# Four ordinary chunks in every Strassen block, and low-weight products behind high-weight ones

## The chip, the cores and the metric

The kernel runs on one core of a Trainium2 chip. The metric is the device time of one execution in microseconds. In the profile PE is TensorE (matmuls), PEld its weight loads, DVE is VectorE, ACT is ScalarE, and SP is the engine whose queue issues the DMAs.

## The reference

A two-layer encoder trunk on 256 tokens of width 2048, all in float32. Each layer has a token mixer (dilated and grouped-query attention in layer 0, latent attention in layer 1) and a channel mixer. Each sub-layer is added to x after a second norm. What matters here is the channel mixer, whose last product is the down projection, 256 x 5632 by 5632 x 2048:

```python
D_MODEL = 2048
SEQ = 256
D_FF = 5632
...
def conv_glu(h, w_up, conv_w, conv_b, w_down):
    u = h @ w_up
    gate, val = u[..., :D_FF], u[..., D_FF:]
    gate = depthwise_conv3(gate, conv_w, conv_b)
    return (jax.nn.gelu(gate, approximate=False) * val) @ w_down
...
    for i in range(DEPTH):
        p = layers[i]
        h = rms_norm(x, p['mix_pre'])
        if i % 2 == 0:
            m = mixer_dilated_gqa(h, *p['mixer'], pos, row, col)
        else:
            m = mixer_mla(h, *p['mixer'], pos)
        x = x + rms_norm(m, p['mix_post'])
        h = rms_norm(x, p['ffn_pre'])
        x = x + rms_norm(conv_glu(h, *p['ffn']), p['ffn_post'])
    return x
```

## The kernel before

**Numbers in two parts.** TensorE multiplies a rounded format, so each float32 operand is held as a high part (its rounding) and a low part (the rest). A product of two such operands is three matmuls into one PSUM bank: high by high, high by low, low by high. `mm3` (lines 227 to 232) issues them: line 230 multiplies the activation's high part by the weight's high part, line 231 the activation's high part by the weight's low part, line 232 the activation's low part by the weight's high part. In the down projection the activations are the stationary operand (128 x 128) and the weights the moving one (512 columns).

**The stream of weights.** All weights of the program form one list of chunks of 128 x 1024 (512 KB), in the order in which they are used. `weights` (line 187) hands out the next chunk, splits up to two chunks further (`_split`, line 159) and loads up to five ahead (`_load`, line 148). A split is a cast on ACT (line 173, `whi`) and, after it, a subtraction on DVE (line 174, `wlo`). There are four buffers for the loaded chunk (`raw`) and three each for `whi` and `wlo`. All loads are issued from SP's queue.

**The down projection** (`down`, lines 1002 to 1129) makes the 2048 output columns in two halves `h`, and each half as two column blocks `o` of 512 by two token halves `t` of 128: four banks of accumulation (`acc`). Along the 5632 rows there are 22 pairs of 256 rows. The pairs from 6 on are done in the ordinary way: one chunk for each pair and `o`, with two row blocks and two token halves, so four products, 12 matmuls. The first six pairs (`PAIRS`) are done by a Strassen scheme: for one pair the 2 x 2 blocks of tokens, rows and columns take seven products instead of eight. Its weights come as two chunks (`seven_a`, `seven_b`, one buffer each), and are used in four steps j = 0 to 3 with 2, 2, 2 and 1 products (6, 6, 6 and 3 matmuls). Step 0 splits `seven_a` as it came. Behind it four subtractions on DVE (`Seven.sums`, line 68, with line 76) turn `seven_a` and `seven_b` in place into differences and fill `seven_t`; step 1 splits the new `seven_a`, step 2 the new `seven_b`, step 3 `seven_t`. The next pair's `seven_a` can be loaded once step 1 has been split, its `seven_b` once step 2 has. The seven sums go to the four ordinary banks and to four more (`at`); at the end of the six pairs `added` and `done` bring them together on ACT and DVE. The sums of tokens that the scheme needs are made on DVE by `sums` (line 1010) while the first chunks run.

**The order.** `down_order(h)` writes it out: `LEAD[h]` ordinary chunks first (6 in the first half, 1 in the second), then for each of the six pairs a block with the four steps and some ordinary chunks among them, then the ordinary chunks left over. For pairs 0 to 3 a block is step 0, two ordinary chunks, step 1, an ordinary chunk, steps 2 and 3, an ordinary chunk. For pairs 4 and 5 it is step 0, two ordinary chunks, steps 1 and 2, an ordinary chunk, step 3. The same list orders the loads (`all_chunks`, line 1152). In the second half the last three ordinary chunks (`HOLD`) are held and run first for t = 0 and then for t = 1, so that the norm can begin.

**Who sets the engines' order.** The framework sorts the instructions of each engine when the program is built: it follows the written order, and puts an instruction that it takes for ready ahead of one that it takes for waiting. Products into one bank keep their order. The order on an engine is fixed when the kernel runs.

`products` (line 1095) issues one step's or chunk's products for one token half; for a Strassen step all are issued in the first call.

Of the kernel before, what the change touches and what calls it, by code (L numbers as in the profile page):

```python
# [31 lines left out]


PAIRS = 6
LEAD = 6, 1


def down_order(h):

    plain = [("plain", p, o) for o in range(2) for p in range(PAIRS, KF // 2)]  # L40
    out, plain = plain[:LEAD[h]], deque(plain[LEAD[h]:])
    for p in range(PAIRS):
        for j in (0, None, None, 1, None, 2, 3, None) if p < 4 else (0, None, None, 1, 2, None, 3):
            out.append(plain.popleft() if j is None else ("seven", p, j))
    return out + list(plain)

# [40 lines left out]
class Model:  # L87
# [914 lines left out]
    def down(self, gh, gl, post, pre):  # L1002

        nc = self.nc
        add = lambda out, a, b, op=ALU.add: nc.vector.tensor_tensor(out=out, in0=a, in1=b, op=op)  # L1005
        mm = self.mm3
        ss = self.small.tile([P, 2, 4], F32, tag="ss", name="ss", bufs=2)
        seven, m, gains = [], [], []

        def sums():  # L1010

            for i in range(PAIRS // 2):
                tmp = self.act.tile([P, 2, 1024], F32, tag="xm3", name="sums")
                add(tmp[:, 0], gh[i].rearrange("p k t -> p (k t)").bitcast(F32),
                    gl[i].rearrange("p k t -> p (k t)").bitcast(F32))
                a = tmp[:, 0].rearrange("p (q k t f) -> p q k t f", q=2, k=2, t=2)
                s = tmp[:, 1].rearrange("p (q n f) -> p q n f", q=2, n=4)
                a11, a12, a21, a22 = (a[:, :, k, t] for t in range(2) for k in range(2))
                add(s[:, :, 0], a21, a22)
                add(s[:, :, 1], s[:, :, 0], a11, ALU.subtract)  # L1020
                add(s[:, :, 2], a11, a21, ALU.subtract)
                add(s[:, :, 3], a12, s[:, :, 1], ALU.subtract)
                yield
                seven.append(self.act.tile([P, 2, 4, 2, P], F32R, tag=f"xm{i}", name=f"seven{i}"))
                self.parted(seven[i][:, :, :, 0, :], seven[i][:, :, :, 1, :], s)
                yield

        def tokens(k, t):
            return tuple(g[k // 4][:, k % 4, t * P:(t + 1) * P] for g in (gh, gl))

        def summed(p, n):
            return tuple(seven[p // 2][:, p % 2, n, i, :] for i in range(2))

        def operands(kind, p, j, t):

            if kind == "plain":
                return [(2 * j + t, lambda k=2 * p + i: tokens(k, t), i) for i in range(2)]
            if t:
                return []
            return [[(4, lambda: tokens(2 * p, 0), 0), (0, lambda: tokens(2 * p + 1, 0), 1)],  # L1040
                    [(5, lambda: summed(p, 0), 0), (1, lambda: tokens(2 * p + 1, 1), 1)],
                    [(7, lambda: summed(p, 2), 0), (2, lambda: summed(p, 3), 1)],
                    [(6, lambda: summed(p, 1), 0)]][j]

        def added(h, at):

            p1, p5, p6, p7 = at
            x = m[h]
            nc.scalar.copy(x[:, 0, 0], p1)
            add(x[:, 1, 0], p6, x[:, 0, 0])  # L1050
            yield
            add(x[:, 0, 1], p7, x[:, 1, 0])
            add(x[:, 1, 0], p5, x[:, 1, 0])
            yield
            add(x[:, 1, 1], p5, x[:, 0, 1])
            yield

        def total(h, o, t):
            x = m[h][:, o, t]
            add(x, banks[2 * o + t], x)  # L1060
            return x

        def scaled(h, o, t):
            x = m[h][:, o, t]
            add(x, x, gains[2 * h + o], ALU.mult)

        def done(h, o, first=None):
            if first:
                yield from first
            for t in range(2):  # L1070
                self.square_sums(ss[:, t, 2 * h + o:2 * h + o + 1], total(h, o, t))
                yield
                scaled(h, o, t)
                yield

        gains.append(self.gain_row(post, 0))
        self.now(sums())
        ended = None
        for h in range(2):
            items = down_order(h)  # L1080
            units = [n for n, item in enumerate(items) if item[0] == "seven"]
            if h == 0:
                gains.append(self.gain_row(post, 1))
            n = len(items) - (HOLD if h else 0)
            todo = [(i, t) for i in range(n) for t in range(2)] + \
                [(i, t) for t in range(2) for i in range(n, len(items))]
            used = [(i, t, *op) for i, t in todo for op in operands(*items[i], t)]
            first, last = {}, {}
            for q, u in enumerate(used):
                first.setdefault(u[2], q)  # L1090
                last[u[2]] = q
            used = deque(enumerate(used))
            banks = self.acc(4)

            def products(i, t, w):
                while used and used[0][1][:2] == (i, t):
                    q, (_, _, b, x, blk) = used.popleft()
                    c = slice(512 * blk, 512 * blk + 512)
                    xh, xl = x()
                    mm(banks[b], xh, xl, w[0][:, c], w[1][:, c], q == first[b], q == last[b])  # L1100

            for i in range(n):
                if i == units[0]:
                    banks += [self.psum("at") for _ in range(4)]
                w = self.weights()
                while items[i][0] == "seven" and len(seven) <= items[i][1] // 2:
                    self.tick()
                for t in range(2):
                    products(i, t, w)
                self.tick()  # L1110
                if i == units[-1]:
                    m.append(self.act.tile([P, 2, 2, 512], F32, tag="xm2" if h else "xm3", name=f"m{h}"))
                    if h:
                        gains.append(self.gain_row(post, 3))
                    ended = self.now(done(h, 0, added(h, banks[4:])))
            if h == 0:
                self.finish(ended)
                gains.append(self.gain_row(post, 2))
                ended = self.now(done(0, 1))
                self.finish(ended)  # L1120
                self.table(AF.Sqrt, ss[:, 0, 1:2])
        self.finish(ended)
        part = self.three(ss)
        ws = [self.weights(self.at + HOLD - j) for j in range(HOLD)]
        for t in range(2):
            for j in range(HOLD):
                products(n + j, t, ws[j])
        self.passage([x[:, o] for x in m for o in range(2)], part, lambda t: total(1, 1, t),
                     lambda t: scaled(1, 1, t), pre)
# [22 lines left out]
    def all_chunks(self):  # L1152
        a = self.a
        groups = lambda w, gs: [w[g, c] for g in gs for c in range(w.shape[1])]
        out = groups(a["w_in0"], [8, 6, 7, 0, 2, 4, 1, 3, 5])
        out += [a["w_out0"][g, c] for g in range(4) for c in (4, 5, 6, 7, 0, 1, 2, 3)]

        def down(w):
            items = []
            for h in range(2):  # L1160
                pairs = [Seven(w[2 * h, p], w[2 * h + 1, p]) for p in range(PAIRS)]
                items += [w[2 * h + j, p] if kind == "plain" else (pairs[p], j) for kind, p, j in down_order(h)]
            return items

        ffn = lambda l: groups(a[f"w_up{l}"], [g for j in range(NFG) for g in (j, NFG + j)]) + \
            down(a[f"w_down{l}"])
        out += ffn(0)
        out += groups(a["w_in1"], [0, 1]) + [a["w_kr"]]
        for p in range(8):
            out += groups(a["w_qr"], [p // 4]) if p % 4 == 0 else []  # L1170
            out += [a["w_qn"][p], a["w_kn"][p]]
            out += groups(a["w_v"], [p // 2]) if p % 2 == 0 else []
        out += groups(a["w_out1"], range(4))
        out += ffn(1)
        return out
# [67 lines left out]
```

## Time and profile before

| | us |
|---|---|
| median of 3 runs | 2081.06 |
| the three runs | 2081.06, 2071.93, 2081.37 |
| profiled execution, its time | 2090.57 |
| profiled execution, its span | 2088.8 |
| granted TensorE clock | 0.999 of full |
| down projection of layer 0, first to last matmul start | 832.01 to 1069.64 |
| down projection of layer 1, first to last matmul start | 1841.76 to 2078.91 |

The span is from the first to the last instruction in one execution taken with the profiler; all durations in this document come from that execution. A row of the timeline has the start in us, the duration, the engine, the line of the kernel, the operation, the output and inputs by the program's names, shapes, and how many like instructions in a row it stands for. In brackets is the idle time ahead of it and what ended that. The end of a matmul is modelled: the next one starts before the shown end.

### The profile page before, as it was taken

How to read it: one execution, taken by the hardware profiler on the slowest of the kernel's cores; microseconds unless marked ns; L12 is line 12 of the kernel's file. 1: busy time of each engine (PE TensorE's matmuls, PEld its weight loads, DVE VectorE, ACT ScalarE, POOL GpSimd, SP SyncE). 2: the span in 40 equal slices, each digit the busy share in tenths (PEclk: the TensorE clock that was granted, in tenths of full speed). 3: DMA queues.
4: the chain of work that ended last, by engine and by line, in shares of the span. 5: the costliest groups of instructions: out<-in, count | busy, mean ns of one | idle time of the engine just before them, and what ended most of it. 6: DMA issues, size and time to landing. Idle time of an engine off the chain costs nothing.

```text
span 2088.8 us, 29118 instructions
## 1 busy us (share of the span) xinstructions
PE 2065.2 (99%) x10905; PEld 1757.4 (84%) x10905; DVE 1479.2 (71%) x2263; ACT 1127.2 (54%) x1753; POOL 0.2 (0%) x4
## 2 busy tenths in 40 slices
PE   9999999999999999999999999999999999999997
PEld 7888888888888888877778998888888888888786
DVE  6876757667667667878786875666666666787776
ACT  6655546555455555555465655555555545554553
POOL 0000000000000000000000000000000000000000
PEclk9999999999999999999999999999999999999999
DMA  8545565665666666666565445666565666556564
GB/s 316 171 151 166 168 203 182 190 190 182 188 187 188 183 188 187 183 201 196 183 192 170 127 127 179 185 198 186 183 189 188 183 190 185 182 181 208 192 205 137
DMA packets 108717, 385.96 MB, mean 185 GB/s; under 512 B 12064, under 2 KB 12576, under 8 KB 108576
## 3 DMA queue, kind: packets, MB, share of 16 engines
q1 hardware_dynamic: 108288, 383.83, 59.1%
q8 instruction: 85, 1.39, 0.3%
q14 instruction: 56, 0.46, 0.1%
q10 hardware_dynamic: 288, 0.28, 0.0%
HBM read 381.96 MB, written 2.10 MB: 184 GB/s over the span
## 4 chain that ended last, share of the span: by engine, by line
PE 94%; DVE 4%; ACT 1%; DMA 1%; issue 1%; DVEq 0%; SPq 0%; ACTq 0%
PE ps L244 32%; PE ps L245 16%; PE ps L231 14%; PE ps L232 14%; PE ps L230 14%; PE ps L537 1%; DVE wlo L174 1%; PE ps L300 1%; ACT whi L173 1%; DVE x L454 1%; DVE seven_a L76 1%; DMA seven_a<-in_w_down 0%; DVE m L1005 0%; DVE seven_t L76 0%; PE ps L478 0%
## 5 line engine op out<-in xcount | busy, mean ns | idle before, releaser
L174 DVE TENSOR_TENSOR wlo<-raw,whi 128x1024 fp32r<-128x1024 f32 (+1 forms) x662 | 808.0, 1222 | 515.2 <-ACT whi L173 512.9
L173 ACT CAST whi<-raw 128x1024 fp32r<-128x1024 f32 (+1 forms) x662 | 693.2, 1049 | 675.6 <-PE ps L244 353.3
L244 PE MATMUL ps<-xhl,whi 128*128 128x512 f32 x2816 | 996.4, 399 | 1.0 <-DVE xhl L591 1.0
L245 PE MATMUL ps<-xhl,wlo 128*128 128x256 f32 x2816 | 789.6, 281 | 0.0
L244 PEld LDWEIGHTS ps<-xhl,whi 128*128 128x128 f32 x2816 | 528.7, 188 | 132.2 <-DVE xhl L591 2.0
L245 PEld LDWEIGHTS ps<-xhl,wlo 128*128 128x128 f32 x2816 | 531.9, 189 | 1.1 <-DVE wlo L174 0.6
L231 PE MATMUL ps<-wlo,gh 128*128 128x512 f32 x584 | 229.8, 394 | 4.7 <-DVE wlo L174 4.4
L232 PE MATMUL ps<-whi,gl 128*128 128x512 f32 x584 | 227.5, 389 | 0.0
L230 PE MATMUL ps<-whi,gh 128*128 128x512 f32 x584 | 223.4, 389 | 0.0
L230 PE MATMUL ps<-whi,xhl 128*128 128x512 f32 x352 | 138.7, 395 | 1.4 <-ACT whi L173 1.4
L231 PEld LDWEIGHTS ps<-wlo,gh 128*128 128x128 f32 x584 | 109.6, 188 | 34.9 <-DVE wlo L174 12.5
L231 PE MATMUL ps<-wlo,xhl 128*128 128x512 f32 x352 | 137.7, 391 | 0.0
L232 PE MATMUL ps<-whi,xhl 128*128 128x512 f32 x352 | 137.3, 390 | 0.0
L230 PEld LDWEIGHTS ps<-whi,gh 128*128 128x128 f32 x584 | 109.6, 188 | 22.9
L232 PEld LDWEIGHTS ps<-whi,gl 128*128 128x128 f32 x584 | 109.7, 188 | 22.0
L230 PE MATMUL ps<-whi,oh 128*128 128x512 f32 x256 | 100.0, 390 | 0.0
L231 PE MATMUL ps<-wlo,oh 128*128 128x512 f32 x256 | 99.7, 389 | 0.0
L232 PE MATMUL ps<-whi,ol 128*128 128x512 f32 x256 | 99.6, 389 | 0.0
L305 ACT COPY half<-ps 128x256 f32<-128x256 f32 x176 | 65.0, 370 | 43.8 <-DVE g L306 18.0
L230 PEld LDWEIGHTS ps<-whi,xhl 128*128 128x128 f32 x352 | 66.0, 188 | 15.0 <-ACT whi L173 1.7
L232 PEld LDWEIGHTS ps<-whi,xhl 128*128 128x128 f32 x352 | 66.1, 188 | 13.9
L231 PEld LDWEIGHTS ps<-wlo,xhl 128*128 128x128 f32 x352 | 66.3, 188 | 13.4 <-DVE wlo L174 0.8
(211 smaller groups left out, 2066.1 us busy)
## 6 DMA issues: line engine op xcount, KB each, us to landing
raw<-in_w_up SPq DMA_DIRECT2D x352, 512.0 KB, 4.1
raw<-in_w_down SPq DMA_DIRECT2D x128, 512.0 KB, 3.8
raw<-in_w_in SPq DMA_DIRECT2D x88, 512.0 KB, 3.9
raw<-in_w_out SPq DMA_DIRECT2D x64, 512.0 KB, 4.1
seven_a<-in_w_down SPq DMA_DIRECT2D x24, 512.0 KB, 4.3
seven_b<-in_w_down SPq DMA_DIRECT2D x24, 512.0 KB, 4.3
gb<-in_post SPq DMA_DIRECT2D x16, 256.0 KB, 3.9
raw<-in_w_qn SPq DMA_DIRECT2D x8, 512.0 KB, 3.6
```

The lines of the kernel that those rows point to most:

```text
L76: nc.vector.tensor_tensor(out=out, in0=x, in1=y, op=ALU.subtract)
L173: self.nc.scalar.copy(hi[:, s], raw[:, s])
L174: self.nc.vector.tensor_tensor(out=lo[:, s], in0=raw[:, s], in1=hi[:, s].bitcast(F32), op=ALU.subtract)
L230: mm(ps, lh, rh, start=start, stop=False)
L231: mm(ps, lh, rl, start=False, stop=False)
L232: mm(ps, ll, rh, start=False, stop=stop)
L244: mm(out[i], hi[:, s], x(k), start=k == 0, stop=False)
L245: mm(out[i][:, :T], lo[:, s], x(k)[:, :T], start=False, stop=k == nk - 1)
L300: self.tc.keep_in_program_order(self.nc.tensor.transpose(out, x, self.ident))
L305: self.nc.scalar.copy(b, ps[:, T:])
L454: return nc.vector.scalar_tensor_tensor(out=x, in0=m[c][:, t, s], scalar=r[t], in1=x, op0=ALU.mult, op1=ALU.add)
L537: nc.tensor.matmul(ps[:, i, :], l, r, start=n == 0, stop=n == len(pairs) - 1))
```

## The change

`LEAD` of the first half goes from 6 to 5. Every block gets the pattern that pairs 0 to 3 had, so pairs 4 and 5 have four ordinary chunks instead of three, with one of them now after step 3. The number of chunks, of products and of loads stays: the ordinary chunks come from the lead (first half) and from the rest behind the blocks, four of which become three in the first half and nine seven in the second.

In `products` the three matmuls of a product are no longer issued together. For one call, first come high by high and low by high (both with the weight's high part) of each product, then high by low (with the weight's low part) of each. An ordinary chunk's call has two products, so four matmuls with `whi` and then two with `wlo`. `mm3` remains in use elsewhere.

```diff
 PAIRS = 6
-LEAD = 6, 1
+LEAD = 5, 1
...
     for p in range(PAIRS):
-        for j in (0, None, None, 1, None, 2, 3, None) if p < 4 else (0, None, None, 1, 2, None, 3):
+        for j in (0, None, None, 1, None, 2, 3, None):
             out.append(plain.popleft() if j is None else ("seven", p, j))
     return out + list(plain)
...
-        mm = self.mm3
+        mm = nc.tensor.matmul
...
             def products(i, t, w):
+                group = []
                 while used and used[0][1][:2] == (i, t):
                     q, (_, _, b, x, blk) = used.popleft()
-                    c = slice(512 * blk, 512 * blk + 512)
-                    xh, xl = x()
-                    mm(banks[b], xh, xl, w[0][:, c], w[1][:, c], q == first[b], q == last[b])
+                    group.append((banks[b], *x(), slice(512 * blk, 512 * blk + 512), q == first[b], q == last[b]))
+                for bank, xh, xl, c, start, _ in group:
+                    mm(bank, xh, w[0][:, c], start=start, stop=False)
+                    mm(bank, xl, w[0][:, c], start=False, stop=False)
+                for bank, xh, _, c, _, stop in group:
+                    mm(bank, xh, w[1][:, c], start=False, stop=stop)
```

## The prediction

> **What bounds the kernel now.** I read the page first: busy shares, then the groups of lines.
>
> ```profile
> span 2088.8 us, 29118 instructions
> ...
> PE 2065.2 (99%) x10905; PEld 1757.4 (84%) x10905; DVE 1479.2 (71%) x2263; ACT 1127.2 (54%) x1753; POOL 0.2 (0%) x4
> ...
> L231 PE MATMUL ps<-wlo,gh 128*128 128x512 f32 x584 | 229.8, 394 | 4.7 <-DVE wlo L174 4.4
> ```
>
> TensorE is the bound; every product has its own weight load (equal counts). A change of order can win only TensorE's idle time in the down projections. The idle column understates it, because a matmul's shown end (0.39 us) lies beyond the next one's start; so I take starts, from the timeline: the first and last product of each down projection, and the first of the nine ordinary chunks that end the second one.
>
> ```profile
> 832.01 0.40 PE L230 MATMUL ps<-whi,gh 128*128 128x512 f32 x1
> ...
> 1069.64 0.39 PE L232 MATMUL ps<-whi,gl 128*128 128x512 f32 x1
> ...
> 1841.76 0.40 PE L230 MATMUL ps<-whi,gh 128*128 128x512 f32 x1
> ...
> 2054.65 0.39 PE L230 MATMUL ps<-whi,gh 128*128 128x512 f32 x1
> ...
> 2078.91 0.39 PE L232 MATMUL ps<-whi,gl 128*128 128x512 f32 x1
> ```
>
> The last nine chunks are 9 x 12 = 108 products, 107 steps in 24.26 us: **0.2267 us each, without a stall**. An ordinary chunk thus takes 2.72 us, a Strassen step 1.36 (the fourth 0.68). One down projection has 64 x 12 + 12 x 21 = 1020 products, 1019 steps, 231.0 us; it lasted 237.6 (layer 0) and 237.2 (layer 1). Lost: 6.6 + 6.1 = 12.7 us. That is all there is to win, 0.6%. The excess of single starts over 0.2267 names 12.1 of it; 0.6 is rounding over 2038 steps.
>
> **Place 1, the ordinary chunk after steps 2 and 3** (timeline, all engines, end of the fourth block):
>
> ```profile
> 862.23 0.50 PE L231 MATMUL ps<-wlo,gh 128*128 128x512 f32 x1
> ...
> 908.48 1.23 DVE L174 TENSOR_TENSOR wlo<-raw,whi 128x1024 fp32r<-128x1024 f32 x1 [2.25 <-ACT whi L173]
> ...
> 909.23 0.61 PE L230 MATMUL ps<-whi,gh 128*128 128x512 f32 x2
> ...
> 909.76 0.50 PE L231 MATMUL ps<-wlo,gh 128*128 128x512 f32 x1
> ...
> 910.32 0.39 PE L230 MATMUL ps<-whi,gh 128*128 128x512 f32 x1
> ...
> 2025.09 0.50 PE L231 MATMUL ps<-wlo,gh 128*128 128x512 f32 x1
> ```
>
> The chunk's low weights are ready at 909.71, 0.48 us after its first product. From 909.23 four steps take 1.09 us instead of 0.91: 0.07 lost ahead of the late product, 0.11 in the two steps behind it (0.56 for 0.45). It recurs in every block of four, four times a half, 16 times in all, the first and the last late product being at 862.23 and 2025.09: 16 x 0.18 = **2.9 us**. The order on TensorE isn't the written one: two high products (L230) run before the first low one (L231), the second of them from the other token half, whose bank differs. The build has already moved ahead what it could; behind L231 everything waits.
>
> **Place 2, the block after one with three ordinary chunks** (pairs 4 to 5, first half of layer 0; timelines of SP, ACT, DVE, PE):
>
> ```profile
> 901.34 0.33 SPq L62 DMA_DIRECT2D seven_a<-in_w_down  x1
> ...
> 908.75 1.06 ACT L173 CAST whi<-seven_a 128x1024 fp32r<-128x1024 f32 x1 [0.30 <-PE ps L232]
> ...
> 917.18 0.33 SPq L62 DMA_DIRECT2D seven_a<-in_w_down  x1
> ...
> 922.04 1.05 ACT L173 CAST whi<-seven_a 128x1024 fp32r<-128x1024 f32 x1 [0.90 <-DMA seven_a<-in_w_down]
> ...
> 926.93 2.35 DVE L174 TENSOR_TENSOR wlo<-raw,whi 128x1024 fp32r<-128x1024 f32 x2
> ...
> 926.44 0.61 PE L230 MATMUL ps<-whi,gh 128*128 128x512 f32 x2
> 928.20 0.50 PE L231 MATMUL ps<-wlo,gh 128*128 128x512 f32 x1 [1.14 <-DVE wlo L174]
> ```
>
> The single buffer seven_a comes free at 901.3 in the block of four, and its cast waits 7.4 us later for TensorE. One block on, with three, the cast waits for the transfer (issue to cast 4.86 us); behind it on DVE come the four differences, then the next chunk's split. Two steps from 926.44 the late product should start, 0.45 us on; it starts 1.76 on: 1.31 lost, with the 0.11 behind it 1.42. The same place in the other three halves:
>
> ```profile
> 1032.12 0.61 PE L230 MATMUL ps<-whi,gh 128*128 128x512 f32 x2
> 1034.14 0.50 PE L230 MATMUL ps<-whi,seven 128*128 128x512 f32 x1 [1.41 <-ACT whi L173]
> ...
> 1936.19 0.61 PE L230 MATMUL ps<-whi,gh 128*128 128x512 f32 x2
> 1937.78 0.50 PE L231 MATMUL ps<-wlo,gh 128*128 128x512 f32 x1 [0.98 <-DVE wlo L174]
> ...
> 2041.77 0.61 PE L230 MATMUL ps<-whi,gh 128*128 128x512 f32 x2
> 2043.38 0.50 PE L230 MATMUL ps<-whi,seven 128*128 128x512 f32 x1 [0.99 <-ACT whi L173]
> ```
>
> By the same reckoning 1.68, 1.25 and 1.27 are lost. Together **5.6 us**.
>
> **Places 3 and 4, the change of halves and the start:**
>
> ```profile
> 954.40 0.61 PE L230 MATMUL ps<-whi,gh 128*128 128x512 f32 x2
> 956.15 0.50 PE L231 MATMUL ps<-wlo,gh 128*128 128x512 f32 x1 [1.14 <-DVE wlo L174]
> ...
> 1964.02 0.61 PE L230 MATMUL ps<-whi,gh 128*128 128x512 f32 x2
> 1965.77 0.50 PE L231 MATMUL ps<-wlo,gh 128*128 128x512 f32 x1 [1.14 <-DVE wlo L174]
> ...
> 852.42 0.62 PE L230 MATMUL ps<-whi,gh 128*128 128x512 f32 x2
> 852.88 0.39 PE L230 MATMUL ps<-whi,seven 128*128 128x512 f32 x1
> 853.41 0.50 PE L231 MATMUL ps<-wlo,gh 128*128 128x512 f32 x1
> ...
> 1863.15 0.50 PE L231 MATMUL ps<-wlo,gh 128*128 128x512 f32 x1
> ...
> 826.50:861.00 34.50, 34.36 (x159) 28.30 (x158) 33.32 (x52) 19.34 (x25) 0.00 (x0) 1.00 0.57 170
> 939.60:957.80 18.20, 17.06 (x75) 13.81 (x75) 17.79 (x24) 11.64 (x18) 0.00 (x0) 1.00 0.53 165
> ```
>
> In the two windows (length; busy PE, PEld, DVE, ACT) DVE is busy 33.3 of 34.5 and 17.8 of 18.2 us: here DVE is the bound for a while. At the change of halves it evacuates sums and forms the next pair's differences; each layer loses 1.75 - 0.45 + 0.11 = 1.41 there: **2.8 us**. At the start it still makes the token sums: after three steps from 852.42 the late product comes 0.31 late, 0.42 with what is behind it, and layer 1 (1863.15) does alike: **0.8 us**. 2.9 + 5.6 + 2.8 + 0.8 = 12.1.
>
> **The change part by part.** No product, split, sum or transfer is added or removed; all keep their durations. *Four chunks in every block:* pairs 4 and 5 get 15.64 us of TensorE work for 12.92. In place 2 what is late comes 1.76 to 2.02 us after the chunk's first product; 2.72 more go ahead of it, while the transfer still starts when seven_a is free. That covers all four with 0.7 to spare, so **5.6 goes**. What is late next there is place 1's chunk, now in six blocks a half. The transfers on SP keep their number and order; a pair's two loads still go out once its predecessor's step 1 and 2 are split, and the ordinary loads they pass in the queue have four buffers. Nothing runs on POOL.
>
> *High products first:* a chunk needs its low weights after four products (0.91 us) instead of one as written, two as built (0.45); if the build again puts the other token half's ready products ahead, after eight (1.81). Place 1 needs 0.48 plus the wait's 0.05: **2.9 goes**, with 0.38 to spare. Place 3 needs 1.75 (954.40 to 956.15): after eight products nothing is left, after four 0.84 each. I take 0, since in every row above the build did take the other half's product ahead; both ends stay in the range. whi is released two products earlier, so casts start up to 0.45 us sooner; wlo one product later (0.23), unfelt, as a split follows its cast by 1.1.
>
> *Lead 5 for 6:* against the change. The first block starts 2.72 us sooner for TensorE, and DVE, which is full, has only one split less before it (1.12: two back to back take 2.35, one 1.23). Place 4's lateness, 853.41 - 852.42 = 0.99, becomes 0.99 + 2.72 - 1.12 = 2.59. With eight products ahead 0.78 remains, with four 1.68, at best 0: I take 0.78 in each layer, 1.6 together, the build's habit being that of the rows above. Cover here is DVE's queue; there is none left until 861. In the second half the last block's end lies one chunk nearer to the held chunks; the evacuation ended with
>
> ```profile
> 2065.25 1.29 DVE L1005 TENSOR_TENSOR m<-m,gb 128x512 f32<-128x512 f32 x2
> ```
>
> while the last chunk's t = 0 products came some 8 us later: a chunk of 2.72 less leaves room, cost 0.
>
> **Sum:** 12.1 - 1.6 = 10.5 us won; at worst 12.1 - 2 x (0.84 + 1.68) = 7.1, at best 12.1. The profiled execution took 2090.57 (its span 2088.8) and would take 2080.1; the runs shown have the median 2081.06, 9.5 below it, so I take the same microseconds from that: **2070.6 us** (2069.0 to 2074.0).
>
> **Rivals.** *(B) The order on TensorE stays what it is:* the build places products itself, and might draw the low ones forward again, so that the second edit does nothing. For it: L230 stands before L231 against the text already. Against: it moved ready work ahead of waiting work, never the reverse. Then place 2 turns into place 1 (5.6 - 4 x 0.18 = 4.9 won), and the start loses the whole 2.72 - 1.12 = 1.6 a layer (3.2): 1.7 won, 2079.4 us.
>
> *(C) Slower: the grouped order costs on every product.* Now a product and the next share their stationary operand (L230, L231); afterwards no neighbours do. The loop before, where they never do, alternates 512 and 256 columns:
>
> ```profile
> 831.30 0.40 PE L244 MATMUL ps<-xhl,whi 128*128 128x512 f32 x1
> ...
> 831.65 0.40 PE L244 MATMUL ps<-xhl,whi 128*128 128x512 f32 x1
> ```
>
> From one 512 to the next, with one of 256 (L245) between, it takes 0.35 us, against 1.5 x 0.2267 = 0.34: 0.01 more at most on a product. On all 2040 that is 20 us, net 10 lost: 2091 us. It decides from 0.005 us a product. Against it: 108 products of the present order fit 0.2267 evenly, though two of three neighbours there already differ in the stationary operand. The Trainium skill speaks for this rival ("TensorE: Matmul & The Clock Gate", Step-by-step): weights stay put across many matmuls, so that they are loaded once. By its load time (128 / 1.2, an estimate of 107 ns) 680 reuses given up would cost 73 us if laid bare. The page of the profile shows no reuse to give up: as many loads as products.
>
> **How the numbers follow.** Forecast (A) 0.74, B 0.20, C 0.06. Changes under 0.5% (10.4 us) can't be told from none for this kernel. A's won time, 7.1 to 12.1 with 10.5 likeliest, straddles this, so a little over half of A counts as faster: 0.40; B and the rest of A are within: 0.54; C is slower: 0.06. The three runs shown spread over 9.4 us, so a median may stray some 5: the range reaches from 2064 to 2081, which takes in A and B and leaves C out.
>
> **What would show it.** Place 2: casts of seven_a after every block wait for PE, never for the DMA; no PE wait over 0.5 us there. Place 1: no excess after steps 2 and 3. PE's rows: four whi products, then wlo. Place 3: under 0.9 us lost. Place 4: more lost than 0.4. Steps still 0.2267. From first to last product 232 to 233.5 us a layer. I'm wrong if wlo is later than 1.8 us anywhere new, if steps lengthen, or if time moves outside the down projections.

## The result, and the profile after

| | before | after |
|---|---|---|
| median of 6 runs, us | 2076.68 | 2062.12 |
| lowest to highest, us | 2071.84 to 2081.46 | 2061.92 to 2071.06 |
| profiled execution, us (span) | 2090.57 (2088.8) | 2061.92 (2060.1) |

The ratio of the times is 0.9938, with a 95% interval of 0.9917 to 0.9958: 0.4 to 0.8% faster. The median lies 14.6 us lower, the profiled span 28.7 us. Neither is the size of the change, because the runs of one kernel stand on levels some 9 us apart: of the six of before three lie at 2072 and three at 2081, and the profiled one at 2091; of the six of after five lie at 2062, one at 2071. Compared level by level, lowest with lowest, the change is worth **9.9 us** (2071.84 to 2061.92).

The page of after, its span, busy shares and the group of low-weight products:

```profile
span 2060.1 us, 29196 instructions
...
PE 2043.4 (99%) x10905; PEld 1750.0 (85%) x10905; DVE 1478.4 (72%) x2263; ACT 1129.3 (55%) x1753; POOL 0.2 (0%) x4
...
L1104 PE MATMUL ps<-wlo,gh 128*128 128x512 f32 x584 | 182.0, 390 | 0.8 <-DVE wlo L174 0.8
```

The wait for low weights in this group has gone from 4.7 to 0.8 us. As before, the whole loss shows in starts. The timeline of after, with the first and last products of the two down projections (line 1101 is high by high, 1102 low by high, 1104 the product with the low weights):

```profile
822.75 0.39 PE L1101 MATMUL ps<-whi,gh 128*128 128x512 f32 x1
...
1054.69 0.61 PE L1104 MATMUL ps<-wlo,gh 128*128 128x512 f32 x2
...
1818.06 0.39 PE L1101 MATMUL ps<-whi,gh 128*128 128x512 f32 x1
...
2049.99 0.61 PE L1104 MATMUL ps<-wlo,gh 128*128 128x512 f32 x2
```

The second product of a row of two starts a step of 0.23 later, so the projections last 232.2 us each, against 237.6 and 237.2: **10.5 us won in the two**. The other 18 us of the 28.7 lie outside: 9.3 before layer 0's down projection (its first product at 822.75 for 832.01) and 9.0 between the two (763.1 us for 772.1). There the up projections run, which the change doesn't touch. Each is a stream of 1408 pairs of a 512-column product (line 244) and a 256-column one (line 245). The same two stretches of 400 us in the window view, first of before (length, PE busy with the number of matmuls, granted clock, DMA share, GB/s):

```profile
400.00:800.00 400.00, 400.00 (x2266) 1.00 0.62 186
1400.00:1800.00 400.00, 400.00 (x2266) 1.00 0.61 187
```

and of after:

```profile
400.00:800.00 400.00, 400.00 (x2309) 1.00 0.62 190
1400.00:1800.00 400.00, 400.00 (x2310) 1.00 0.62 190
```

At the same granted clock, with PE busy throughout, the pair takes 2 x 400 / 2266 = 0.353 us in the one trace and 0.3465 in the other. Over 1408 pairs 6.7 ns make 9.4 us, about the distance of the levels (the first 64 pairs of a layer run unevenly in both traces). So a layer's up projection has two rates, and the levels are 0, 1 or 2 layers at the slower one. The trace of before, from the highest level, has two slow layers, that of after, from the lowest, none. Whether the change had a hand in that was the first question for the experiments.

The four places of the prediction, in after. Place 1, the ordinary chunk after steps 2 and 3, with DVE's split of its low weights:

```profile
911.53 1.23 DVE L174 TENSOR_TENSOR wlo<-raw,whi 128x1024 fp32r<-128x1024 f32 x1 [2.25 <-ACT whi L173]
...
912.74 0.39 PE L1101 MATMUL ps<-whi,gh 128*128 128x512 f32 x1
...
913.65 0.62 PE L1104 MATMUL ps<-wlo,gh 128*128 128x512 f32 x2
```

The low weights are ready at 912.76 and wanted at 913.65, four even steps after the first product; before, they were wanted sooner than they came. The chunk stands in the fifth block, where before had none at this point. In place 2, at the same point, seven_a's cast for the sixth block waits on ACT for TensorE and no longer for its transfer:

```profile
911.81 1.05 ACT L173 CAST whi<-seven_a 128x1024 fp32r<-128x1024 f32 x1 [0.31 <-PE ps L1102]
```

Places 4 (the start) and 3 (the change of halves) keep a small loss:

```profile
837.74 0.39 PE L1101 MATMUL ps<-whi,gh 128*128 128x512 f32 x1
...
839.33 0.39 PE L1102 MATMUL ps<-whi,gl 128*128 128x512 f32 x1
839.62 0.50 PE L1101 MATMUL ps<-whi,seven 128*128 128x512 f32 x1
839.96 0.40 PE L1102 MATMUL ps<-whi,seven 128*128 128x512 f32 x1
840.73 1.20 PE L1104 MATMUL ps<-wlo,gh 128*128 128x512 f32 x4 [0.37 <-DVE wlo L174]
841.76 0.40 PE L1101 MATMUL ps<-whi,gh 128*128 128x512 f32 x1
...
946.10 0.39 PE L1101 MATMUL ps<-whi,gh 128*128 128x512 f32 x1
...
946.77 0.39 PE L1102 MATMUL ps<-whi,gl 128*128 128x512 f32 x1
947.12 0.73 PE L1104 MATMUL ps<-wlo,gh 128*128 128x512 f32 x2
947.69 0.39 PE L1101 MATMUL ps<-whi,gh 128*128 128x512 f32 x1
```

From 839.33 to 841.76 there are seven steps, 1.59 us; it took 2.43, so 0.84 is lost at the start. From 946.77 to 947.69 three steps took 0.92: 0.24 lost at the change of halves. Ahead of 840.73 ten high products ran from 837.74 on, eight of the chunk and two of the next Strassen step: here the build drew the other token half's products ahead. It did so at few places. In place 1 and in place 3 (946.10 to 946.77) only the four written ones stand ahead of the low products.

### The profile page after: what moved, and what is told of

It reads as the page before. It is cut to its first block, busy times and chain, and to the rows that moved or that the text cites. A ratio compares the mean times of both kernels' runs of the same rounds, so it can differ in the third digit from the quotient of the medians.

```text
span 2060.1 us, 29196 instructions
## 1 busy us (share of the span) xinstructions
PE 2043.4 (99%) x10905; PEld 1750.0 (85%) x10905; DVE 1478.4 (72%) x2263; ACT 1129.3 (55%) x1753; POOL 0.2 (0%) x4
## 4 chain that ended last, share of the span: by engine, by line
PE 96%; DVE 3%; issue 0%; ACT 0%; DMA 0%; DVEq 0%; SPq 0%; ACTq 0%
PE ps L244 31%; PE ps L245 16%; PE ps L230 8%; PE ps L231 8%; PE ps L232 8%; PE ps L1104 7%; PE ps L1101 7%; PE ps L1102 7%; PE ps L537 1%; PE ps L300 1%; DVE x L454 1%; DVE wlo L174 1%; PE ps L478 0%; DVE sums L1005 0%; DMA raw<-in_w_in 0%
## 5 line engine op out<-in xcount | busy, mean ns | idle before, releaser
L244 PE MATMUL ps<-xhl,whi 128*128 128x512 f32 x2816 | 978.7, 394 | 1.0 <-DVE xhl L591 1.0
L245 PE MATMUL ps<-xhl,wlo 128*128 128x256 f32 x2816 | 779.2, 277 | 0.0
L1104 PE MATMUL ps<-wlo,gh 128*128 128x512 f32 x584 | 182.0, 390 | 0.8 <-DVE wlo L174 0.8
```

The source lines that it names most:

```text
L244: mm(out[i], hi[:, s], x(k), start=k == 0, stop=False)
L245: mm(out[i][:, :T], lo[:, s], x(k)[:, :T], start=False, stop=k == nk - 1)
L1104: mm(bank, xh, w[1][:, c], start=False, stop=stop)
```

## The experiments

Two questions: which edit wins what in the down projections, and what sets the rate of the up projections. My theory: the change is worth 10.5 us, all of it in the down projections, and the pair rate is drawn by chance in each layer of each execution. The main rival: the change brings the fast rate, and is worth more.

**e1, the first edit alone.**

```diff
-LEAD = 6, 1
+LEAD = 5, 1
...
-        for j in (0, None, None, 1, None, 2, 3, None) if p < 4 else (0, None, None, 1, 2, None, 3):
+        for j in (0, None, None, 1, None, 2, 3, None):
```

> Four ordinary chunks in every block and lead 5, products in the old order. My theory: the two down projections last 474.8 us before and 464.3 after; of the 10.5 won, this edit alone keeps the wins of place 2 (5.6) but pays place 1 in 24 places for 16 (+1.4) and the start (+3.2): 1 to 2 us won, 473 to 474 us in the two. The up projections show 353.3 or 346.7 ns a pair in each layer, by chance. Rival 1 (the blocks are what matters): 5 us or more won in the two. Rival 2 (the change brings the fast pair rate): with one edit alone the rate stays 353.3 in both layers.

Measured: 2075.07 us median of 10 (2070.34 to 2088.45), ratio 0.9997 (0.9972 to 1.0022). The timeline has the down projections' ends:

```profile
823.00 0.39 PE L230 MATMUL ps<-whi,gh 128*128 128x512 f32 x1
...
837.98 0.61 PE L230 MATMUL ps<-whi,gh 128*128 128x512 f32 x2
839.83 0.50 PE L230 MATMUL ps<-whi,seven 128*128 128x512 f32 x1 [1.23 <-ACT whi L173]
...
1059.48 0.39 PE L232 MATMUL ps<-whi,gl 128*128 128x512 f32 x1
...
1822.70 0.39 PE L230 MATMUL ps<-whi,gh 128*128 128x512 f32 x1
...
2059.17 0.39 PE L232 MATMUL ps<-whi,gl 128*128 128x512 f32 x1
```

236.5 us each, 473.0 together: 1.8 won, as expected. The start shows why so little: from the first of the two products at 837.98 to the one at 839.83 are two steps (0.45), and 1.85 passed, so 1.4 are lost, 1.5 with the late step behind it, against 0.4 before. The wait here ended with ACT's cast of seven_a, and not with low weights. Both up projections ran at the fast rate, so the fast rate does not need the second edit:

```profile
400.00:800.00 400.00, 400.00 (x2310) 1.00 0.63 190
1400.00:1800.00 400.00, 400.00 (x2309) 1.00 0.64 190
```

**e2, the second edit alone** (`products` as in the change, `LEAD` and the blocks as before).

> Products with whi first, blocks and lead as before. My theory: eight products of cover take place 1 (2.9), the start (0.8), most of the change of halves (2.3) and most of place 2 (late by 1.8 to 2.0, covered by 1.8), so 10.5 to 11.5 us are won in the two down projections, as much as by both edits: 463.3 to 464.3 us. Rival 1 (the blocks are what matters): place 2 keeps its 5.6, 6 us won, 469 us. Rival 2 (the change brings the fast pair rate): 353.3 ns in both layers here, or always 346.7 if it is this edit.

Measured: 2062.92 us median of 10 (2062.18 to 2071.93), ratio 0.9934 (0.9908 to 0.9960). The timeline's ends, with the only wait over 0.3 us that was left in layer 0, and the two windows:

```profile
831.71 0.40 PE L1101 MATMUL ps<-whi,gh 128*128 128x512 f32 x1
...
1027.50 0.39 PE L1101 MATMUL ps<-whi,gh 128*128 128x512 f32 x1
...
1028.41 0.39 PE L1101 MATMUL ps<-whi,gh 128*128 128x512 f32 x1
1029.30 0.73 PE L1104 MATMUL ps<-wlo,gh 128*128 128x512 f32 x2 [0.50 <-DVE wlo L174]
...
1063.88 0.61 PE L1104 MATMUL ps<-wlo,gh 128*128 128x512 f32 x2
...
1827.60 0.39 PE L1101 MATMUL ps<-whi,gh 128*128 128x512 f32 x1
...
2059.49 0.61 PE L1104 MATMUL ps<-wlo,gh 128*128 128x512 f32 x2
```

```profile
400.00:800.00 400.00, 400.00 (x2266) 1.00 0.62 186
1400.00:1800.00 400.00, 400.00 (x2309) 1.00 0.63 190
```

232.4 and 232.1 us: 10.3 won of the 10.5 of both edits (10.5 to 11.5 was expected). The rival by which the blocks matter falls. But the cover was not the eight products that were expected: in place 2 five high products stand ahead of the low ones (1027.50 to 1028.41), 1.13 us, and the first low product came 1.13, 1.80, 1.27 and 1.25 us after the chunk's first one in the four places, earlier than in before. They still lose 1.4 us together, 0.77 of it at 1029.30. In one execution layer 0 ran at the slow rate and layer 1 at the fast one: the rate belongs to a layer, and not to the kernel.

**e3, both edits with the lead of 6.**

```diff
-LEAD = 5, 1
+LEAD = 6, 1
```

> Both edits, but the lead of the first half stays 6 (two ordinary chunks left over behind its blocks, not three). My theory: the start, late by 0.99 and covered by 1.81, loses nothing: 0.8 a layer less than after, 1.6 in all, 462.7 us in the two down projections; if the shorter rest behind the blocks uncovers the change of halves, 1 us of it comes back there. Rival: the start's loss of 0.8 is not set by the lead; 464.3 us as after. The pair rate: by chance by my theory, 346.7 in both layers by rival 2.

Measured: 2069.41 us median of 9, ratio 0.9959 (0.9933 to 0.9984); the runs are 2060.6 to 2060.8 (three), 2069.3 to 2069.8 (four) and 2078.3 to 2078.5 (two).

```profile
831.88 0.40 PE L1101 MATMUL ps<-whi,gh 128*128 128x512 f32 x1
...
1063.13 0.61 PE L1104 MATMUL ps<-wlo,gh 128*128 128x512 f32 x2
...
1835.34 0.40 PE L1101 MATMUL ps<-whi,gh 128*128 128x512 f32 x1
...
2066.61 0.61 PE L1104 MATMUL ps<-wlo,gh 128*128 128x512 f32 x2
```

231.5 us each, 463.0 together (462.7 expected), 0.7 less in a layer than after. So the lead is what costs at the start, all but 0.16 a layer. The profiled execution had both layers at the slow rate (2266 products in either window), though it has both edits. With e1 this ends the rival by which the change brings the fast rate.

**e4, the stream of pairs broken 44 times.** After, with

```diff
         out = [self.psum(tag) for _ in range(4)]
+        mm(out[0][:, :64], self.zeros[:, :P], self.zeros[:, :64], start=True, stop=True)
         for c in range(nk // 2):
```

> After, with one product of 64 columns of zeros ahead of each of the 22 groups of 64 pairs in each up projection (into a bank that the next product clears). My theory: the pair rate of the up projection is drawn when the stream of matmuls is broken and holds until it is broken again, so both rates, 346.7 and 353.3 ns, stand among the 44 groups, each constant within a group, and the time lies between after's and before's: 2062 to 2081 us. Rival 2 (the change brings the fast rate): 346.7 in all 44. Rival 3 (the rate is drawn once for an execution or layer, by something outside the matmuls): one rate in all 22 groups of a layer.

Measured: 2068.31 us in the one run. In both layers the second group of 64 pairs ran at the slow rate and all twenty behind it at the fast one. Windows of 20 us in layer 0's second, third, fourth and last group:

```profile
358.00:378.00 20.00, 20.00 (x115) 1.00 0.60 180
381.00:401.00 20.00, 20.00 (x117) 1.00 0.62 190
403.00:423.00 20.00, 20.00 (x117) 1.00 0.62 190
781.00:801.00 20.00, 20.00 (x118) 1.00 0.62 185
```

The rate changes at a short product and nowhere else, so that part holds. But it isn't a new draw each time: 40 groups in a row fast is not chance. In both layers a short product ended the slow rate. That could be put to use. The short product differs from the others in more than its width: its zeros are bf16, and no run tells which of this matters.

**e5, e7 and e8: two short products for each up projection**, ahead of the two groups of its second pass, in e3 (e5), in before (e7) and in after (e8).

```diff
-    def proj_t(self, nk, x, tag):
+    def proj_t(self, nk, x, tag, short=False):
...
+        if short:
+            mm(out[0][:, :64], self.zeros[:, :P], self.zeros[:, :64], start=True, stop=True)
...
-                pg = self.proj_t(KD, x, "acc")
+                pg = self.proj_t(KD, x, "acc", gi == 1)
...
-                pv = self.proj_t(KD, x, "at")
+                pv = self.proj_t(KD, x, "at", gi == 1)
```

> Both edits, lead 6, and one product of 64 columns of zeros ahead of each of the two groups of the second pass (gi = 1) of each up projection: four in all, of about 0.12 us each in e4. My theory: the stream of pairs runs at 346.7 ns from there in every run whatever it was before, so all times stand within 1 us of 2061 us (2060.6, e3's lowest, plus 0.5) with no second and third level 9 us higher. Rival: the rate is drawn by something the short products don't set, and levels near 2061, 2070 and 2079 us appear as in e3.

> Before, with the same four short products. My theory: all times at one level, 2072.3 (lowest of before) plus 0.5 = 2072.8 us, the profile's up projections at 346.7 ns and its down projections at 474.8 us as before. Rival: levels of 2072, 2081 and 2090 us as in before.

> After, with the same four short products. My theory: all times at one level, 2062.1 plus 0.5 = 2062.5 us; so against e7, with the pair rate held, the change is worth 10.3 us (10.46 in the two down projections), not the 14.6 us between the medians first measured. Rival (the change also acts on the up projections): more than 12 us between e7 and e8.

Measured, each on one level:

| | runs | median, us | lowest to highest |
|---|---|---|---|
| e5 (lead 6) | 6 | 2062.07 | 2061.86 to 2062.22 |
| e7 (before) | 12 | 2073.60 | 2073.03 to 2074.69 |
| e8 (after) | 7 | 2063.42 | 2063.30 to 2063.69 |

With the rate held, the change is worth 2073.60 - 2063.42 = **10.2 us** (10.3 expected): the rival by which it acts on the up projections falls. All three stand about 1.3 us above the lowest level of their kernels, where 0.5 was expected. In e5 one group after another, again in 20 us (the second and third in layer 0 are those behind the first and the second short product):

```profile
379.00:399.00 20.00, 20.00 (x115) 1.00 0.62 187
402.00:422.00 20.00, 20.00 (x118) 1.00 0.59 184
424.00:444.00 20.00, 20.00 (x117) 1.00 0.61 185
```

The group ahead of the first short product was fast (117 in 358 to 378). That short product made the stream slow for one group (115), and the next brought it back. A slow group of 64 pairs costs 0.4 us, so one in each layer makes up the 0.8 us by which the sum was too low. In e8's layer 0 it went otherwise: slow ahead of the first short product (115), fast behind it (118), and still fast behind the second (117).

**e6, another order of the pairs.** e3 with the high products of both row blocks first, then the two low ones.

```diff
-                for kk in range(2):
-                    k = 2 * c + kk
-                    s = slice(kk * 512 + i * P, kk * 512 + (i + 1) * P)
-                    mm(out[i], hi[:, s], x(k), start=k == 0, stop=False)
-                    mm(out[i][:, :T], lo[:, s], x(k)[:, :T], start=False, stop=k == nk - 1)
+                s = [slice(kk * 512 + i * P, kk * 512 + (i + 1) * P) for kk in range(2)]
+                for kk in range(2):
+                    mm(out[i], hi[:, s[kk]], x(2 * c + kk), start=c + kk == 0, stop=False)
+                for kk in range(2):
+                    mm(out[i][:, :T], lo[:, s[kk]], x(2 * c + kk)[:, :T], start=False, stop=2 * c + kk == nk - 1)
```

> Both edits, lead 6, no short product, but in the up projections the two row blocks' high products (512 columns) come first and then the two low ones (256 columns). Theory A (the slow rate is a cycle of three pairs that lives on the strict alternation of wide and narrow products): it can't form, two pairs take 693.3 ns in both layers in every run, times near 2060.6 us only. Theory B (a wide product behind a narrow one is what costs): with half as many such neighbours the two rates lie closer, 693 and 700 ns, levels 4.5 us apart. Theory C (the order doesn't matter): levels 9 us apart as in e3.

Measured: 2065.97 us median of 10 (2065.82 to 2066.15), ratio 0.9940 (0.9918 to 0.9963): one level, as theory A has it, but not at its time. Both windows of its trace:

```profile
400.00:800.00 400.00, 400.00 (x2298) 1.00 0.63 189
1400.00:1800.00 400.00, 400.00 (x2298) 1.00 0.63 189
```

A pair takes 0.348 us in both layers, between the two rates, and all ten runs agree. With this order in the whole stream the two levels are gone; but it costs 1.7 ns a pair, 4.9 us in 2816 pairs, over the fast rate.

**e9 and e10, to set the rate for less**, both on e3. e9 gives e6's order to one chunk of each layer (the first of the pass gi = 1); e10 puts the two short products 8 pairs apart.

```diff
+                part = [(0, 0), (1, 0), (0, 1), (1, 1)] if mixed and c == 0 else [(0, 0), (0, 1), (1, 0), (1, 1)]
+                for kk, low in part:
```

```diff
             hi, lo = self.weights()
+            if short and c < 2:
+                mm(out[0][:, :64], self.zeros[:, :P], self.zeros[:, :64], start=c == 0, stop=c == 0)
```

> Both edits, lead 6, no short product; in each up projection one chunk (the first of the pass gi = 1) has e6's order, two wide and then two narrow products, all others the old one. My theory: the slow cycle can't live through that chunk, and the stream behind it starts at 346.7 ns: one level of times near 2060.7 us. Rival: what follows is drawn anew by chance, and levels near 2061, 2070 and 2079 us appear as in e3.

> Both edits, lead 6, and two short products of 64 columns close together, ahead of the first and of the second chunk of the pass gi = 1 (not a group of 64 pairs apart as in e5). My theory: in e5 the first short product sent a fast stream into the slow rate for one group (354.5 ns) and the second sent it back; with 8 pairs between them that detour costs 0.1 us instead of 0.5, so one level of times near 2061.1 us (2060.6 plus four products of 0.12). Rival: the second short product draws by chance, and some runs stand 9 us higher.

e9: 2060.88 us median of 9, five runs at 2060.5 to 2060.9 and four at 2069.4 to 2069.7. The levels of its rival came. In its trace layer 0 was fast and layer 1 slow ahead of the changed chunk, and both stayed so behind it. The slow rate thus lived through the chunk, against the theory; that the rate is drawn anew behind it, as the rival has it, is not what this trace shows. e10: **2061.41 us** median of 6 (2061.22 to 2061.61; 2061.1 expected), one level; ratio to before 0.9925 (0.9903 to 0.9948). It stands 0.8 us above e3's lowest level, its highest run lies below after's lowest, and the mean of its runs is the lowest of all versions.

## Why the prediction was right or wrong

**Wrong: the time, 2062.12 against 2070.6, and outside 2064 to 2081.** The step that failed is the last of the sum: "The profiled execution took 2090.57 ... the runs shown have the median 2081.06, 9.5 below it, so I take the same microseconds from that". The 9.5 us were one layer's up projection at the slow rate, and 2081.06 still held another. The profiled execution was two levels above the lowest, the median run one. From the lowest run shown, 2071.93, the same 10.5 us lead to 2061.4. The range failed with it: "a median may stray some 5" took half the spread of three runs for noise, where the times stand on levels and a median can lie on any of them. In the six traces without short products and with the pairs in their old order (before, after, e1, e2, e3, and e9, where one chunk differs) the level of the time goes by the number of slow layers; runs without a trace are counted by their time alone. The runs of before in all comparisons bear that out (67; a single one of 4925.6 us isn't counted): 33 near 2072, 29 near 2081, 5 near 2090. If each layer is slow by itself with the chance 39 / 134 = 0.29, one expects 34, 28 and 6. After's one slow layer in twelve is luck that e3, which has both edits, didn't have (8 in 18). The prediction's own sign, "if time moves outside the down projections", came up: 18 us moved there between the two traces, by the rate and not by the change.

The clue was in the prediction. Rival C put the pair of lines 244 and 245 at 0.01 us more than 1.5 steps and asked what this would cost if the down projections caught it. That the up projections were paying it, 2816 times (half of it even at the fast rate), and that a run 9 us faster had to lack something, was not asked.

**Right: the change itself.** Predicted 10.5 us of 12.1 named (7.1 to 12.1); measured 10.5 in the traces and 10.2 with the rate held. By the places it is 10.0 (12.1 before, 2.1 after); the other 0.4 lies in steps that were longer by less than 0.02 us each, which the prediction took for rounding. That the sum agrees to a tenth is luck in part, as the places show.

- Place 1: gone in 16 places (2.9) and not there in the eight new ones; e1 shows 0.18 in each of twelve in a layer.
- Place 2: nothing is left (5.6 won). But the price was counted for one edit where either could pay: the second edit alone takes all but 1.4 of it (e2), with five high products ahead and a lateness of 1.13 to 1.80 (1.59 to 2.02 in the rows of before). Why the low weights come earlier there than in before, no run was made to show.
- Place 3: 0.24 a layer is left where 0 was taken and 0.84 bounded it. Both premises were off: four products stand ahead and not eight ("the build did take the other half's product ahead" fails here), and the low product comes 1.02 after the chunk's first (946.10 to 947.12) and not 1.75.
- Place 4: 0.84 a layer is left, 0.78 predicted. That near agreement is luck in part: the low product comes 2.99 after the chunk's first (837.74 to 840.73) and not 2.59, ten products stand ahead and not eight, and 0.18 of the loss is the late high weights of the Strassen step (839.62 and 839.96). e3, with the lead of 6, loses 0.16 there: the lead of 5 is the cause.

**The rivals.** B, that the build takes the new order back, fell: in the rows shown a chunk's whi products stand ahead of its wlo ones. Its sum (1.7 us won by the blocks alone) is near what e1 measured, 1.8, but by two errors that cancel: place 1 is paid in eight more places and not in four (1.4 for 0.7), and the start cost 1.1 a layer more and not 1.6. C, a dearer step, fell: four steps from 912.74 take 0.91 us, as before, though no neighbours share the stationary operand now. The Trainium skill's one load for many matmuls ("TensorE: Matmul & The Clock Gate", Step-by-step) is not what these traces show, before or after: each product has a load of its own, of 0.19 us and not the estimated 107 ns, which runs beside a product.

**What the edits are worth**, in the two down projections: order alone 10.3 us, blocks and lead alone 1.8, both 10.5, both without the new lead 11.8. Four ordinary chunks in each block add 1.5 to the order, and the shorter lead takes 1.4 of that back. Where DVE is full, at the start, a chunk less of TensorE work isn't an economy.

## What to carry to other kernels

Where two engines prepare the operands of a product, run first what needs only the first engine's part: with mostly four or five matmuls of cover the order alone won 10.3 of the 10.5 us of both edits. When two edits cover the same wait, don't add their gains: ask of each what it takes alone. And before taking a sum from a median, look whether the runs stand on levels; a stage that the change doesn't touch may hold more than the change is worth.

## What the runs showed of the hardware that was not expected

A steady stream of matmuls that alternates 512 and 256 columns, with a new stationary operand each time, keeps one of two rates for 450 us on end, 0.353 or 0.3465 us a pair, at a granted clock of 1.00 and with PE never idle. The rate is settled early in each layer, differently from one execution of the same program to the next: without short products, and counted by the level of each run, 61 of 222 layers were slow. Two products of 64 columns, 8 or 64 pairs apart, left the fast rate in all 62 layers of e5, e7, e8 and e10; one alone could turn a fast stream slow.

The starts of the wide products, in ns, show three steady patterns. The slow stream repeats 349, 350, 361. The fast one either alternates 350 and 343, as in after, or stays even at 347, 347, 346, as in e4 from its third group on; both make 0.3467 us on average. In the traces of e4, e5, e7, e8 and e10 a short product made the slow stream fast in 10 of 10 cases, made the alternating one slow in 6 of 6, and left the even one as it was in 40 of 40 (cases where the stream was steady ahead of it). So in these traces two in a row ended fast from either start, and one alone need not; that they always must is not shown.

The Trainium skill gives N / 2.4 + 2.5 ns for the isolated gap of a warm matmul ("TensorE: Matmul & The Clock Gate", Back-to-back issue gap), by which a pair would take 325 ns (an estimate). Both measured rates are longer. What the patterns are inside the engine, and why a short product changes them, no run here shows.
